# Larger pieces for kept depthwise outputs, half-height band loads, and a schedule that counts a transfer's packets

## The chip, the core and the metric

The kernel runs on one core of one Trainium2 chip, in one launch. The metric is the device time of an execution in microseconds (us); the kernel before takes 2142.71 us (median of three runs). Engines are named as in the profile: PE is TensorE, whose weight loads (PEld) overlap its matmuls, DVE is VectorE, ACT is ScalarE, POOL is GpSimd, and SP is SyncE, which issues every DMA of this program.

## What is computed

The program is a decoder trunk of two layers over 1024 tokens of width 1024, all in float32. Layer 0 mixes tokens with a causal convolution module, layer 1 with windowed attention. Each layer then has a squared-ReLU MLP and a gated embedding. The change lies in the convolution module:

```python
def conformer_conv(x, w_in, b_in, w_dw, b_dw, ln_g, ln_b, w_out, b_out):
    h = x @ w_in + b_in
    a, gate = jnp.split(h, 2, axis=-1)
    h = a * jax.nn.sigmoid(gate)
    h = lax.conv_general_dilated(
        h, w_dw[:, None, :], window_strides=(1,), padding=[(CONV_WIDTH - 1, 0)],
        dimension_numbers=("NWC", "WIO", "NWC"), feature_group_count=D_MODEL) + b_dw
    h = jax.nn.silu(layer_norm(h, ln_g, ln_b))
    return h @ w_out + b_out
...
        x = layer_norm(DEEPNORM_ALPHA * x + y, mix_ln_g[i], mix_ln_b[i])
        x = layer_norm(DEEPNORM_ALPHA * x + sq_relu_mlp(x, mlp_w_up[i], mlp_w_down[i]),
                       mlp_ln_g[i], mlp_ln_b[i])
        x = x + (p[i] @ ple_w_proj[i]) * jax.nn.sigmoid(x @ ple_w_gate[i])
```

The depthwise convolution has 31 taps (CONV_WIDTH) for each of 1024 channels.

## The kernel before

**Precision and products.** Every operand is split in two parts (`wh`/`wl` for weights, `xh`/`xl` for activations), a rounded one that ACT writes and the rest that DVE writes. A product is three matmuls (`mm3`).

**The convolution stage.** Channels are worked in eight groups `c` of 128. For each group `conv_in(c)` multiplies by `w_in` (for `c` from 3 on by `conv_seven(c)`, seven half products in place of eight), applies the gate and calls `hand_over(c, h, g)` for each half `h` of the tokens: the gated half is split into a `zz` tile (for the last half of the last group a `wh` tile) and written to scratch memory `scr` in eight DMAs of 64 KB. `taps(c)` then does the depthwise convolution on PE. For each of two halves `jj` of the group's channels it loads two tiles `B` back from `scr`, and for each of them two bands of weights from `w_dw`. A band comes through a `z` tile of 576 columns. ACT rounds it into a band tile `E`, DVE writes the remainder for partitions 0 to 63 beside it, and nine matmuls of 256 columns use the two (in the profile `ps<-B,E`). There are 64 bands. The host lays each band out twice, for partitions 0 to 63 and again for 64 to 127.

**Kept outputs.** After a half group, four transposes bring its result into a PSUM tile `tr` with tokens on partitions. For the first seven groups (`c < KEPT`) one copy moves it to a `t` tile, on DVE for `jj` 0 and on ACT for `jj` 1, and one DMA writes that to `kept` in DRAM, 2 KB for each partition. At group 7 the outputs come back in 16 DMAs into tiles `X` (groups 0 to 3) and `A` (groups 4 to 6), one for each of the eight token tiles and each of the two. `kept` is ordered by group, half and token tile, so such a read collects pieces of 64 elements (256 bytes).

**What follows.** `conv_ln` takes the statistics of each token tile on DVE, normalizes on POOL (`X<-X,sm` and `A<-A,sm` in the profile), transposes on PE and applies Silu on ACT. `mix_out` multiplies by `w_out`. The embedding product `embed(0, ...)`, 96 matmuls which depend on none of this (`ps<-wh,wh`, `ps<-wl,wh`, `ps<-wh,wl`), stands between the taps and `conv_ln` in the program and is spread over both.

**Who sets the order.** The program is recorded as a list of operations, and `Recorder.schedule` writes each engine's instruction order from it by list scheduling: priorities follow the order of recording, shifted by `later`, and each operation gets a planned duration (`cost`). For a DMA the plan has one queue. A transfer begins 1400 ns after its issue at the earliest, occupies the queue for its elements divided by 75 ns, and its data are there 2800 ns after the issue at the earliest. Tiles come from pools with few slots (`SLOTS`: 4 of `z`, 5 of `t`, 1 of `zz`, 6 of `ps`, 2 of `tr`); an operation that needs a slot waits until the slot's last user is done. On the chip each engine runs its order as written and waits at semaphores, so what stands behind a waiting instruction on its engine waits too. The DMAs use eight completion semaphores in turn, so SP issues a DMA only when the one eight places earlier has landed. All operations are recorded through one line, L466 (L471 in the changed kernel), so the profile is read by tile names.

Of the kernel before, what the change touches and what calls it, by code (L numbers as in the profile page):

```python
# [10 lines left out]
F32 = mybir.dt.float32  # L11
F32R = mybir.dt.float32r
AF = mybir.ActivationFunctionType
ALU = mybir.AluOpType

P = 128
# [4 lines left out]
HT = 512  # L21
# [11 lines left out]
PH = 4  # L33
# [19 lines left out]
KEPT = 7  # L53
# [69 lines left out]
class View:  # L123
# [30 lines left out]

    def to_broadcast(self, shape):
        return View(self.buf, np.broadcast_to(self.idx, shape[1:]), self.parts, self.steps + (("bro", shape),))

    def real(self):
        a = self.buf.tile
# [37 lines left out]
class Recorder:  # L197
# [120 lines left out]
    def schedule(self):  # L318
        import heapq

        for o in self.ops:
            o.deps.pop(o, None)
            o.left = len(o.deps)
            for x in o.deps:
                x.outs.append(o)
        engs = ("tensor", "vector", "scalar", "gpsimd", "sync")

        held = dict(vector=0.0, gpsimd=0.0)

        def both(o):  # L330
            if o.eng == "gpsimd":
                return o.name != "memset" and o.outv[0].n > 8
            if o.eng != "vector":
                return False
            if o.name == "tensor_copy":
                src = o.allv
            else:
                src = [v for k, v in o.kw.items() if k in ("in0", "in1") and isinstance(v, View)]
            return len(src) > 1 and not any(v.buf.space == "PSUM" for v in src)

        free = dict.fromkeys(engs, 0.0)
        fut = {e: [] for e in engs}
        rdy = {e: [] for e in engs}
        table = 0
        dma = 0.0
        order = []
        lat = 200.0
        same = dict(vector=127.0, scalar=93.0, gpsimd=100.0)

        def delay(o, x):  # L350
            a, b = o.eng, x.eng
            if a in ("alloc", "sync") or b == "alloc":
                return 0.0
            if a == b:
                return same.get(a, 0.0)
            return 200.0 if a == "tensor" else 260.0 if b == "tensor" else 150.0

        def enable(o):
            if o.eng == "alloc":
                return  # L360
            for e in ("vector", "gpsimd") if o.eng == "either" else (o.eng,):
                heapq.heappush(fut[e], (o.ready, o.prio, o.num, o))

        def finish(o, end):
            o.end = end
            order.append(o)
            for x in o.outs:
                r = end + delay(o, x) + (0.0 if o.eng in ("tensor", "alloc") else x.slack)
                if r > x.ready:
                    x.ready = r  # L370
                x.left -= 1
                if x.left == 0:
                    enable(x)
            for b in o.bufs:
                b.users -= 1
                b.end = max(b.end, end)
                if b.users == 0 and b.slot is not None:
                    heapq.heappush(self.tags[b.tag]["free"], (b.end + lat, b.slot))
                    serve(b.tag)

        def serve(tag):
            t = self.tags[tag]
            q = t["queue"]
            while q and t["free"]:
                o = q.pop(0)
                ft, s = heapq.heappop(t["free"])
                o.alloc.slot = s
                if o.name == "move":
                    dst = o.args[1]
                    heapq.heappush(self.tags[dst]["free"], (ft, s))  # L390
                    finish(o, ft)
                    serve(dst)
                else:
                    finish(o, ft)

        for o in self.ops:
            if o.eng == "alloc":
                self.tags[o.alloc.tag]["queue"].append(o)
        for t in self.tags:
            serve(t)  # L400
        for o in self.ops:
            if o.left == 0 and o.eng != "alloc" and not o.deps:
                enable(o)
        while True:
            best = None
            for e in engs:
                while rdy[e] and rdy[e][0][2].end:
                    heapq.heappop(rdy[e])
                while fut[e] and fut[e][0][3].end:
                    heapq.heappop(fut[e])  # L410
                if rdy[e]:
                    t = free[e]
                elif fut[e]:
                    t = max(free[e], fut[e][0][0])
                else:
                    continue
                if best is None or t < best[0]:
                    best = (t, e)
            if best is None:
                break  # L420
            t, e = best
            while fut[e] and fut[e][0][0] <= t:
                r, p, i, o = heapq.heappop(fut[e])
                if not o.end:
                    heapq.heappush(rdy[e], (p, i, o))
            p, i, o = heapq.heappop(rdy[e])
            if WAIT and fut[e] and e != "tensor":
                r, p2, i2, o2 = fut[e][0]
                if not o2.end and r <= t + WAIT and p2 < p - 300:
                    heapq.heappush(rdy[e], (p, i, o))  # L430
                    heapq.heappop(fut[e])
                    t, o = r, o2
            if o.eng == "either":
                o.eng = e
                o.dur = self.cost(o, o.outv, o.allv)
            d = o.dur
            if e == "scalar" and o.name == "activation":
                k = TABLE.get(o.args[2].name if len(o.args) > 2 else "", 0)
                if k and k != table:
                    table = k  # L440
                    d += 1283.0
            if both(o):
                d += max(0.0, held["gpsimd" if e == "vector" else "vector"] - 50.0 - t)
                held[e] = t + d
            free[e] = t + d
            if e == "sync":
                v = o.allv[0]
                dma = max(dma, t + 1400.0) + v.n * v.parts / 75.0
                finish(o, max(dma, t + 2800.0))
            else:  # L450
                finish(o, t + d)
        assert len(order) == len(self.ops), (len(order), len(self.ops))
        self.length = max(free.values())
        return order
# [44 lines left out]
class Emit:  # L499
# [318 lines left out]
    def conv(self):  # L818

        nc, d, ws = self.nc, self.d, self.ws  # L820
# [13 lines left out]
        Z = {}  # L834
# [138 lines left out]
        def taps(c):  # L973
# [3 lines left out]
            for jj in range(2):  # L977
                pss = [self.ps() for k in range(2)]
                for j in range(2):
# [3 lines left out]
                    nc.sync.dma_start(G2[:, :, HIST : HIST + U], scr[c, 2 * jj + j].rearrange("p (k u) -> p k u", k=2))  # L983
                    exchange = nc.ops[-1]
                    for k in range(2):
                        w = nc.tile("z", (P, n))
                        nc.sync.dma_start(w, d["w_dw"][c, jj, 2 * j + k])
                        w = w.rearrange("p (m q) -> p m q", q=PH * CG)
                        e = bands[turn[0] % len(bands)]
# [2 lines left out]
                        if e in fresh:  # L992
                            fresh.remove(e)
                            nc.gpsimd.memset(ev.bitcast(F32)[LOW, :, 1, :], 0.0)
                        nc.scalar.copy(ev[:, :, 0, :], w)
                        nc.vector.tensor_tensor(
                            out=ev[HIGH, :, 1, :], in0=w[HIGH], in1=ev[HIGH, :, 0, :].bitcast(F32), op=ALU.subtract
                        )
                        for i in range(SHIFTS):
                            o = k * LO + HIST - i  # L1000
# [23 lines left out]
                        nc.tensor.transpose(pv[:, h, j], y[:, o : o + P], self.ident)  # L1024
                nc.slack = 0.0
                if c < KEPT:
                    s = self.sb("t")
                    (nc.scalar.copy if jj else nc.vector.tensor_copy)(s, pt)
                    nc.sync.dma_start(kept[:, (2 * c + jj) * HT : (2 * c + jj + 1) * HT], s)
                    yield  # L1030
                    continue
                if c == KEPT and jj == 0:
                    kv = kept.rearrange("p (c s u) -> p c s u", c=2 * KEPT, s=2 * PH)
                    for q in range(2):
                        m = min(8, 2 * KEPT - 8 * q)
                        for h in range(2):
                            for f in range(PH):
                                Z[h, f, q] = self.sb("XA"[q])
                                dst = Z[h, f, q][:, 0 : 64 * m].rearrange("p (c u) -> p c u", u=64)
                                with nc.later(BACK_BY):  # L1040
                                    nc.sync.dma_start(dst, kv[:, 8 * q : 8 * q + m, PH * h + f, :])
                for h in range(2):
                    for f in range(PH):
                        o = c % 4 * P + jj * 4 * CG
# [43 lines left out]
            forms()  # L1088
        more_bands()
        kept = self.dram("kept", 2 * KEPT * HT)  # L1090
        ins = (x for c in range(8) for x in conv_in(c))
        outs = (x for c in range(8) for x in taps(c))
        for n in range(32 + LAG):
# [902 lines left out]
def layout(a):  # L1996
# [9 lines left out]
    r = {}  # L2006
# [21 lines left out]
    for q in range(CG):  # L2028
        band[:, :, :, :, q, :, q] = wt[:, :, :, :, q, :]
    band = band.reshape(8, 2, 4, P // 2, SHIFTS * PH * CG)  # L2030
    r["w_dw"] = c(np.concatenate([band, band], axis=3))

    bd = np.asarray(a["conv_b_dw"])[0].reshape(32, 2, CG).transpose(2, 1, 0).reshape(CG, 64)
    r["cconst"] = c(
# [45 lines left out]
```

## Time and profile before

| | before |
|---|---|
| median of 3 runs | 2142.71 us (2142.64 to 2142.78) |
| the profiled execution's own time | 2142.3 us |
| its span in the trace | 2140.5 us |
| PE busy | 2116.5 us, 99% |
| DVE, ACT, POOL busy | 1757.5, 1152.3, 280.6 us |
| moved by DMA | 462.46 MB in 228939 packets, mean 216 GB/s |
| packets under 512 bytes | 38192 |

The span runs from the first to the last instruction of one profiled execution; the execution's own time has 1.8 us around that. Busy time of PE is the union of its matmuls, each of which is drawn with its full latency (389 ns for 512 columns) although the next one starts after some 226 ns; a short delay between two matmuls therefore does not show as idle time.

### The profile page before, as it was taken

What the parts mean: (1) busy time and instruction counts of PE and PEld (TensorE: products, weight loads), DVE (VectorE), ACT (ScalarE), POOL (GpSimd) and SP (SyncE); (2) the same over time, 40 slices, a digit from 0 to 9 for tenths busy, and PEclk for the clock granted to TensorE, in tenths of its full rate; (3) what the DMA queues carried; (4) which work ended last, traced back from release to release, by engine and by line L of the source; (5) the groups of instructions that cost most, each with busy time, mean ns of one, the idle gap of its engine ahead of it and who ended that gap; (6) DMA issues with size and microseconds to landing.
All of it is one profiled execution on the core that took longest, in us unless ns stands there. A gap on an engine that the chain in (4) does not pass through costs nothing.

```text
span 2140.5 us, 29992 instructions
## 1 busy us (share of the span) xinstructions
PE 2116.5 (99%) x10008; PEld 1752.9 (82%) x10008; DVE 1757.5 (82%) x2854; ACT 1152.3 (54%) x2146; POOL 280.6 (13%) x495
## 2 busy tenths in 40 slices
PE   9999899999999999999999999999999999999999
PEld 7888778888888888888788888888888888888877
DVE  6866579988898788876986888689988988788688
ACT  5655554654544633335755888445445554333484
POOL 0000052200000000001320656240000000000042
PEclk9999999999999999999999999999999999999999
DMA  9877965867786756655487022665778795565726
GB/s 295 234 203 203 268 245 177 285 222 250 264 271 231 278 177 204 201 184 213 156 284 249 11 89 79 208 239 184 257 267 296 262 332 174 179 233 170 262 75 230
DMA packets 228939, 462.46 MB, mean 216 GB/s; under 512 B 38192, under 2 KB 64432, under 8 KB 228784
## 3 DMA queue, kind: packets, MB, share of 16 engines
q1 hardware_dynamic: 228784, 460.54, 65.1%
q8 instruction: 79, 1.29, 0.2%
q14 instruction: 76, 0.62, 0.1%
HBM read 312.34 MB, written 148.11 MB: 215 GB/s over the span
## 4 chain that ended last, share of the span: by engine, by line
PE 40%; DVE 5%; ACT 3%; DMA 2%; issue 1%; POOL 1%; SPq 0%; POOLq 0%; DVEq 0%; ACTq 0%
PE ps L466 31%; PE tr L466 9%; DVE xl L466 1%; DMA t<-proj 1%; ACT z L466 1%; DVE t L466 1%; POOL sm L466 1%; DVE z L466 1%; DVE sm L466 0%; DVE A L466 0%; DVE B L466 0%; ACT xh L466 0%; DMA raw<-in_w_kv_dram 0%; ACT t L466 0%; DMA raw<-gate_t 0%
## 5 line engine op out<-in xcount | busy, mean ns | idle before, releaser
L466 PE MATMUL ps<-xh,xl 128*128 128x512 f32 x636 | 247.6, 389 | 0.0
L466 PE MATMUL ps<-xh 128*128 128x512 f32 x636 | 247.6, 389 | 0.0
L466 PE MATMUL ps<-xl,xh 128*128 128x512 f32 x636 | 247.6, 389 | 0.0
L466 ACT CAST wh<-raw 128x1024 fp32r<-128x1024 f32 (+2 forms) x156 | 143.4, 923 | 134.7 <-PE ps L466 84.0
L466 POOL TENSOR_SCALAR sm<-sm 128x1 f32<-128x1 f32 x72 | 28.3, 397 | 1364.0 <-DVE E L466 612.0
L466 PE MATMUL ps<-xl,wh 128*128 128x512 f32 x508 | 198.7, 392 | 0.0
L466 PE MATMUL ps<-xh,wl 128*128 128x512 f32 x508 | 198.3, 391 | 0.0
L466 PE MATMUL ps<-xh,wh 128*128 128x512 f32 x508 | 196.1, 392 | 0.9 <-ACT xh L466 0.9
L466 PE MATMUL ps<-wh,xh 128*128 128x512 f32 (+1 forms) x404 | 159.2, 395 | 1.7 <-ACT zz L466 0.9
L466 PE MATMUL ps<-wh,xl 128*128 128x512 f32 (+1 forms) x404 | 160.4, 397 | 0.0
L466 PE MATMUL ps<-wl,xh 128*128 128x512 f32 (+1 forms) x404 | 159.3, 394 | 0.0
L466 ACT CAST wh<-g 128x512 fp32r<-128x512 f32 x128 | 76.4, 620 | 153.8 <-PE ps L466 73.7
L466 ACT CAST xh<-wh 128x1024 fp32r<-128x1024 f32 x76 | 79.7, 1049 | 118.0 <-PE tr L466 90.4
L466 PEld LDWEIGHTS ps<-xl,xh 128*128 128x128 f32 x636 | 119.4, 188 | 24.9
L466 PEld LDWEIGHTS ps<-xh,xl 128*128 128x128 f32 x636 | 119.4, 188 | 24.7
L466 PEld LDWEIGHTS ps<-xh 128*128 128x128 f32 x636 | 119.5, 188 | 24.6
L466 DVE TENSOR_TENSOR wl<-raw,wh 128x1024 fp32r<-128x1024 f32 (+1 forms) x100 | 100.0, 1001 | 35.5 <-ACT wh L466 35.1
L466 DVE TENSOR_TENSOR xl<-wh,xh 128x1024 fp32r<-128x1024 f32 x76 | 92.8, 1221 | 25.6 <-ACT xh L466 25.6
L466 PEld LDWEIGHTS ps<-xh,wh 128*128 128x128 f32 x508 | 95.4, 188 | 22.5 <-ACT xh L466 1.6
L466 PEld LDWEIGHTS ps<-xh,wl 128*128 128x128 f32 x508 | 95.5, 188 | 19.5
L466 PEld LDWEIGHTS ps<-xl,wh 128*128 128x128 f32 x508 | 95.4, 188 | 19.5 <-DVE xl L466 1.3
L466 DVE TENSOR_TENSOR wl<-g,wh 128x512 fp32r<-128x512 f32 x128 | 84.6, 686 | 26.8 <-ACT wh L466 26.8
(447 smaller groups left out, 5620.0 us busy)
## 6 DMA issues: line engine op xcount, KB each, us to landing
wh<-hid SPq DMA_DIRECT2D x78, 512.0 KB, 4.1
raw<-in_w_up_dram SPq DMA_DIRECT2D x61, 512.0 KB, 4.3
wl<-in_w_down_dram SPq DMA_DIRECT2D x58, 512.0 KB, 4.8
hid<-zz SPq DMA_DIRECT2D x96, 256.0 KB, 4.0
z<-in_w_dw_dram SPq DMA_DIRECT2D x64, 288.0 KB, 4.0
hid<-t SPq DMA_DIRECT2D x70, 256.0 KB, 3.0
raw<-hid SPq DMA_DIRECT2D x30, 512.0 KB, 3.7
B<-scr SPq DMA_DIRECT2D x32, 256.0 KB, 4.5
```

What stands on the lines that cost most here:

```text
L466: getattr(getattr(nc, o.eng), o.name)(*a, **k)
```

## The change

Four things change in the kernel, and the order of all engines with them.

1. A band is laid out once by the host (64 rows) and loaded once, into a `z` tile of 64 partitions. ACT copies it twice, to partitions 0 to 63 (`HIGH`) and to 64 to 127 (`LOW`) of the band tile.
2. A kept output is copied from PSUM in two halves (`h` 0 on DVE, `h` 1 on ACT), into two `t` tiles that are taken at `jj` 0 and filled at `jj` 1. Two DMAs for each group then write them, in pieces of 128 elements (512 bytes), to a `kept` that is ordered by token tile, group and channel.
3. The 16 reads of `kept` are then one contiguous run for each partition (2048 or 1536 bytes).
4. `schedule` charges a transfer by the larger of its two sides: 9 ns for each contiguous piece and 0.0366 ns for each byte, over 16 engines.

```diff
+    def transfer(self):
+
+        i = self.idx.ravel()
+        pieces = self.parts * (1 + int((np.diff(i) != 1).sum()))
+        return (9.0 * pieces + 0.0366 * 4 * i.size * self.parts) / 16
...
             if e == "sync":
-                v = o.allv[0]
-                dma = max(dma, t + 1400.0) + v.n * v.parts / 75.0
+                dma = max(dma, t + 1400.0) + max(v.transfer() for v in o.allv)
                 finish(o, max(dma, t + 2800.0))
...
-                        w = nc.tile("z", (P, n))
+                        w = nc.tile("z", (P // 2, n))
                         nc.sync.dma_start(w, d["w_dw"][c, jj, 2 * j + k])
...
-                        nc.scalar.copy(ev[:, :, 0, :], w)
+                        for rows in (HIGH, LOW):
+                            nc.scalar.copy(ev[rows, :, 0, :], w)
                         nc.vector.tensor_tensor(
-                            out=ev[HIGH, :, 1, :], in0=w[HIGH], in1=ev[HIGH, :, 0, :].bitcast(F32), op=ALU.subtract
+                            out=ev[HIGH, :, 1, :], in0=w, in1=ev[HIGH, :, 0, :].bitcast(F32), op=ALU.subtract
                         )
...
                 if c < KEPT:
-                    s = self.sb("t")
-                    (nc.scalar.copy if jj else nc.vector.tensor_copy)(s, pt)
-                    nc.sync.dma_start(kept[:, (2 * c + jj) * HT : (2 * c + jj + 1) * HT], s)
+                    for h in range(2):
+                        if jj == 0:
+                            wait[h] = self.sb("t")
+                        v = wait[h].rearrange("p (f j u) -> p f j u", f=PH, j=2)
+                        src = pt[:, h * 256 : (h + 1) * 256].rearrange("p (f u) -> p f u", f=PH)
+                        (nc.scalar.copy if h else nc.vector.tensor_copy)(v[:, :, jj, :], src)
+                        if jj:
+                            dst = kept.rearrange("p (s c u) -> p s c u", s=2 * PH, c=KEPT)
+                            nc.sync.dma_start(dst[:, PH * h : PH * h + PH, c, :], wait[h].rearrange("p (f u) -> p f u", f=PH))
                     yield
                     continue
                 if c == KEPT and jj == 0:
-                    kv = kept.rearrange("p (c s u) -> p c s u", c=2 * KEPT, s=2 * PH)
                     for q in range(2):
-                        m = min(8, 2 * KEPT - 8 * q)
+                        m = min(4, KEPT - 4 * q)
                         for h in range(2):
                             for f in range(PH):
                                 Z[h, f, q] = self.sb("XA"[q])
-                                dst = Z[h, f, q][:, 0 : 64 * m].rearrange("p (c u) -> p c u", u=64)
+                                o = ((PH * h + f) * KEPT + 4 * q) * P
                                 with nc.later(BACK_BY):
-                                    nc.sync.dma_start(dst, kv[:, 8 * q : 8 * q + m, PH * h + f, :])
+                                    nc.sync.dma_start(Z[h, f, q][:, 0 : P * m], kept[:, o : o + P * m])
...
-    r["w_dw"] = c(np.concatenate([band, band], axis=3))
+    r["w_dw"] = c(band)
```

More of the change, by code (lines that the diff above doesn't have):

```diff
@@ L1090, in conv @@
         kept = self.dram("kept", 2 * KEPT * HT)
+        wait = {}
         ins = (x for c in range(8) for x in conv_in(c))
```

## The prediction

> **What bounds the kernel now.** I read the busy times first, then the same by stretches of 100 us, since a share over the whole span would hide a bad stage.
>
> ```profile
> span 2140.5 us, 29992 instructions
> PE 2116.5 (99%) x10008; PEld 1752.9 (82%) x10008; DVE 1757.5 (82%) x2854; ACT 1152.3 (54%) x2146; POOL 280.6 (13%) x495
> ```
>
> ```profile
> 0.00:100.00 100.00, 97.02 (x479) 81.12 (x480) 76.34 (x117) 59.91 (x101) 3.56 (x20) 1.00 0.87 265
> 200.00:300.00 100.00, 91.57 (x517) 77.44 (x516) 66.00 (x119) 58.10 (x110) 25.73 (x38) 0.98 0.96 290
> 500.00:600.00 100.00, 100.00 (x443) 82.42 (x442) 89.59 (x141) 50.91 (x87) 0.00 (x0) 1.00 0.79 259
> 1000.00:1100.00 100.00, 96.75 (x462) 78.78 (x462) 85.93 (x147) 70.23 (x126) 33.73 (x40) 1.00 0.46 159
> 2000.00:2140.50 140.50, 134.22 (x630) 110.43 (x628) 109.82 (x178) 85.56 (x147) 38.72 (x43) 0.99 0.55 186
> ```
>
> The columns after the stretch and its length are busy us (and instructions) of PE, PEld, DVE, ACT and POOL, the granted PE clock, the DMA share and GB/s. PE bounds the kernel: it idles 2140.5 - 2116.5 = 24.0 us in all. In a full stretch it starts 443 matmuls of 512 columns, one every 100/443 = 0.226 us. The change removes no matmul, so it can win only idle time. Of that 8.4 us lie in 200 to 300, at the end of the convolution stage, the fullest stretch for DMA (0.96) and the place where the kept outputs return. The next two views take it apart.
>
> ```profile
> 220.00:230.00 10.00, 10.00 (x61) 8.80 (x60) 6.65 (x11) 5.58 (x8) 1.33 (x4) 1.00 1.15 263
> 230.00:240.00 10.00, 7.51 (x49) 6.69 (x48) 8.13 (x12) 5.35 (x11) 0.00 (x0) 0.84 1.00 290
> 240.00:250.00 10.00, 7.04 (x30) 5.23 (x31) 6.13 (x9) 6.11 (x11) 0.00 (x0) 0.98 0.91 246
> 270.00:280.00 10.00, 8.16 (x45) 6.21 (x45) 8.75 (x24) 6.87 (x13) 9.67 (x14) 1.00 0.95 329
> 280.00:290.00 10.00, 9.11 (x49) 6.74 (x48) 6.93 (x13) 7.34 (x15) 9.51 (x13) 1.00 1.04 399
> ```
>
> ```profile
> PE ps L466 <- ACT xh L466: 2.5, 2, 1.6
> PE ps L466 <- DVE E L466: 2.1, 2, 1.1
> PE ps L466 <- POOL X L466: 1.8, 1, 1.8
> PE ps L466 <- DVE g L466: 1.7, 2, 1.2
> PE tr L466 <- POOL X L466: 1.0, 3, 0.4
> ```
>
> The second view lists whom PE waited for in the first 320 us (total, times, longest). There are two troughs. At 230 to 250 PE loses 2.49 + 2.96 = 5.45 us, to bands (`E`) and to the evacuation queue; at 270 to 290 it loses 1.84 + 0.89 = 2.73 us to POOL's normalization. With the 3 us of the first stretch, all within the change's direct reach is some 11 us, half a per cent.
>
> The trough also costs clock: 0.84 granted over 10 us is (1 - 0.84) x 10 / 0.5 = 3.2 us at half speed, 1.6 us of work lost. The Trainium skill ("TensorE: Matmul & The Clock Gate", Part 1) says that the clock halves after an idle window of about 3.4 us, in steps of such windows; the trace agrees with the size of one step, though the longest single wait here is under 2 us. By that rule a longer wait would cost at least the same step again; I charge it once below from the row.
>
> **The change, part by part.**
>
> *Reads of `kept` and band loads.* The reads go from 256-byte pieces to one run; each band load halves.
>
> ```profile
> z<-in_w_dw_dram SPq DMA_DIRECT2D x12, 288.0 KB, 4.4
> B<-scr SPq DMA_DIRECT2D x8, 256.0 KB, 4.9
> kept<-t SPq DMA_DIRECT2D x4, 256.0 KB, 4.6
> scr<-wh SPq DMA_DIRECT2D x8, 64.0 KB, 2.2
> ```
>
> These are landings at 210 to 270 us. The stretch 220:230 moves 263 GB/s at a share of 1.15, 229 GB/s per full share; 280:290, with long pieces only, moves 399 at 1.04, 384. The 16 reads (8 of 256 KB, 8 of 192 KB, 3.67 MB) therefore free about 3.67/0.229 - 3.67/0.384 = 6.5 us of DMA time. A band load of 144 KB should land between the rows of 64 and 288 KB, at about 2.2 + (80/224) x 2.2 = 3.0 us, 1.4 us sooner. With that and the freed queue the 2.1 us of waits for `E` go. Before this trough DMA time hides behind PE, so the saved band bytes win nothing more there.
>
> *ACT's second copy.*
>
> ```profile
> 20.00:250.00 230.00, 223.98 (x1237) 193.80 (x1236) 165.51 (x242) 132.32 (x232) 5.37 (x32) 0.99 0.82 235
> L466 ACT CAST E<-z 128x576 fp32r<-128x576 f32 x64 | 42.6, 667 | 14.6 <-DMA z<-in_w_dw_dram 8.8 <-PE ps L466 3.0 <-PE tr L466 2.3
> L466 DVE TENSOR_TENSOR E<-z,E 64x576 fp32r<-64x576 f32 x64 | 47.2, 746 | 39.4 <-ACT E L466 26.9 <-PE ps L466 12.3
> ```
>
> DVE's band operation takes 746 ns on 64 partitions, so I charge a half-height copy in full: 64 x 0.667 = 42.6 us, bringing ACT from 132.3 to 174.9 of 230 us (76%). DVE needs only the HIGH copy, so the LOW one (667) runs beside DVE's 746 and a band is ready no later. I take 0, with +4 us as the bound if ACT's slack doesn't hold. The 14 evacuations become 28 of half width, split as before: nothing on PE.
>
> *Kept writes.* Two `t` tiles of five stay taken for a whole half group, and the gate's activation of the next group waits for a slot that the write must free, with ACT's bands and casts behind it. In ACT's new order three to five operations stand between (about 2 to 3.3 us at 0.62 to 0.67) against a landing of 4.6; PE has work. 0 here, in a rival below.
>
> *The tail of the taps.* Here the order changes, which I read from the built programs. Both run 54 band matmuls after the last convolution product. Before, 36 embedding matmuls (one of them behind the transposes) follow and then the last group's 72 band matmuls in a row. Now only 10 embedding matmuls stand ahead, the other fillers later.
>
> ```profile
> 222.25 5.31 SPq L466 DMA_DIRECT2D X<-kept  x4
> 228.74 4.46 PE L466 MATMUL ps<-B,E 128*128 128x256 f32 x36
> 230.84 3.95 SPq L466 DMA_DIRECT2D kept<-t  x1
> 232.18 0.67 DVE L466 TENSOR_TENSOR t<-t,ps 128x512 f32<-128x512 f32 x1
> 232.89 0.69 DVE L466 TENSOR_TENSOR t<-t,t 128x512 f32<-128x512 f32 x1
> 233.62 0.62 ACT L466 CAST wh<-t 128x512 fp32r<-128x512 f32 x1 [0.36 <-DVE t L466]
> 234.88 0.68 DVE L466 TENSOR_TENSOR wh<-t,wh 128x512 fp32r<-128x512 f32 x1
> 236.34 4.31 SPq L466 DMA_DIRECT2D scr<-zz  x8
> 241.22 3.71 SPq L466 DMA_DIRECT2D scr<-wh  x8
> 246.89 1.89 SPq L466 DMA_DIRECT2D B<-scr  x3
> 252.07 8.77 PE L466 MATMUL ps<-B,E 128*128 128x256 f32 x72
> ```
>
> Before, SP is held twice (5.31 and 3.95 us), and the last tiles `B` are asked for 18 us after the last product. The chain's parts are the hand-over (0.67 + 0.69 + 0.62 + 0.68 = 2.7, with hops about 3.5), sixteen issues (4.31 + 3.71 = 8.0) and a landing (4.9): the first `B` is there 16.4 us after the product, or 6.8 + 8.0 + 4.9 = 19.7 if the hand-over is as late as before (235.56 - 228.74). PE gets there after 54 x 0.122 + 10 x 0.226 + 0.5 = 9.4 us. So the trough of 5.45 us becomes one wait of 7.0 us, up to 10.3; if the emptier queue lands `B` as fast as `scr` (2.2), 4.3. I take 6.0, and the clock's 1.6 as before: +0.5 us, from -2.8 to +5.
>
> *Normalization.* Taps and POOL move forward together. Before its first transposes PE has 22 fillers after the last tap transposes in place of 28 (6 x 0.226 = 1.4 us less cover), then 31 in place of 26 among the next 32 transposes (1.1 more). I take +0.5 (from -2.7, the whole idle, to +3).
>
> *The start.* The plan now believes in faster transfers, and the first band stands after 176 matmuls, not 221.
>
> ```profile
> 41.40 3.96 SPq L466 DMA_DIRECT2D scr<-zz  x8
> 47.49 2.61 SPq L466 DMA_DIRECT2D B<-scr  x4
> 55.16 2.31 PE L466 MATMUL ps<-B,E 128*128 128x256 f32 x18
> ```
>
> That is 45 x 0.226 = 10.2 us earlier, at 45.0. The product it depends on ends 29 matmuls (6.5 us) earlier, so `B` is asked for at 41.0 and lands at 45.9: PE waits 0.9 us. If `B` isn't asked for earlier at all (47.49 + 4.9 - 45.0), 7.4. I take +1.0 (0 to +7.4).
>
> *The rest.* Attention (1000 to 1400) is reordered too, as its plan starts from other times; the MLP's PE order hardly changes, and PE is full there. I see no sign: 0, within 3 us either way (idle is 3.25 us in 1000:1100, 6.3 in the last stretch).
>
> The sum is 0.5 + 0.5 + 1.0 = +2 us, with the 0.5 that I lean toward loss in the rest, +2.5: a profiled execution of 2142.3 + 2.5 = 2144.8. The median lies 0.4 us above the profiled time, so **2145.2 us**.
>
> **The rivals.** What a measurement of this kernel tells from no change I set at 0.2%, 4.3 us: faster is below 2138.4, slower above 2147.0.
>
> *The relief wins.* Waits for `E` go, SP is never held, `B` lands early, and taps and POOL run forward with more filler behind them. For it: DMA at or over a full share exactly where PE idles. Against it: the fillers are spent later. It gives 2.8 us in the tail, 2.7 us in normalization and 1 us more if the clock never drops, about -6: 2137. Chance 0.18.
>
> *Hidden anyway.* The reads are smaller transfers beside a full PE, and the new order happens to fit; troughs of the same size in other places: 2142.5, within 2. Chance 0.12.
>
> *The plan trusts DMA too far (slower).* One mechanism: band matmuls stand ahead of the time when their `B` tiles land, and PE cannot pass them. At both ends at the bounds: 7.4 at the start, 10.3 + 1.6 - 7.05 = 4.9 at the tail: +12, 2155. It decides from about 2 us of lateness at both ends over my values. For it: shares of 0.87 to 1.15 at both places, so a plan by undisturbed packets is too early there. Half of it gives 2149. Chance 0.28.
>
> *ACT (slower).* At 76%, with the seven waits for kept writes of up to 2 us each (14 us) it would be at 189 of 230, and PE would wait some 0.6 us for each of seven groups and the 0 to 4 us above: +6, 2149. Against it: ACT's longest waits now are for PE, not the other way. Chance 0.10.
>
> **How the numbers follow.** My forecast has 0.32 (2142 to 2148 by itself). Faster is the first rival, 0.18; same is the forecast and the hidden case, 0.44; slower is the last two, 0.38. The range runs from the relief's value to the slow rival's, short of its extreme: 2137 to 2154, leaving out somewhat under 0.2.
>
> **What would show it.** Right: in the changed profile no waits of PE for `E` near 230, the last 72 band matmuls starting near 245 after one wait of 4 to 7 us with the clock below 1 there, ACT near 175 us between 20 and 250, a first band between 45 and 47, and PE's idle sum near 26. Wrong: a PE without troughs up to 310 (relief), PE waiting for ACT in the middle of the stage (ACT), or an idle sum that grows most in 1000 to 1400, which I gave no sign.

## The result, and the profile after

| | before | after |
|---|---|---|
| median | 2142.68 us | 2195.18 us (2188.93 to 2199.58, 4 runs) |
| profiled execution: own time, span | 2142.3, 2140.5 us | 2196.05, 2194.2 us |
| PE busy, idle | 2116.5, 24.0 us | 2135.2, 59.0 us |
| time in which PE's granted clock is 0.5 | 7.9 us | 33.6 us |

The changed kernel is slower by 2.4% (ratio 1.0243, 95% interval 1.0218 to 1.0268). The forecast was 2145.2 us in a range of 2137 to 2154. The time lies 41 us above that range. The page of the changed kernel begins:

```profile
span 2194.2 us, 30087 instructions
PE 2135.2 (97%) x10008; PEld 1761.5 (80%) x10008; DVE 1760.6 (80%) x2856; ACT 1194.6 (54%) x2217; POOL 290.5 (13%) x500
DMA packets 217932, 453.03 MB, mean 206 GB/s; under 512 B 23856, under 2 KB 58288, under 8 KB 217776
```

DVE's work is unchanged (1760.6 against 1757.5 us) and ACT's grew by the 42 us that were forecast. DMA moves 9.4 MB less, in fewer small packets. The work is as planned, so the time is in the waits. The span grew by 53.7 us. PE idle grew by 35.0. The clock accounts for at most (33.6 - 7.9) / 2 = 12.9 us of PE's longer busy time (part of the half-speed time falls into waits or behind the last matmul), and the other 5.8 or more are delays too short to show as idle time. The stretches of the changed kernel (columns as in the prediction) tell where:

```profile
0.00:100.00 100.00, 89.52 (x414) 74.36 (x415) 66.37 (x102) 62.41 (x105) 3.45 (x19) 0.95 0.75 216
200.00:300.00 100.00, 87.22 (x502) 74.84 (x501) 61.19 (x107) 69.79 (x129) 15.37 (x31) 0.97 0.85 248
500.00:600.00 100.00, 100.00 (x441) 82.39 (x441) 88.81 (x141) 50.60 (x86) 0.00 (x0) 1.00 0.75 250
1100.00:1200.00 100.00, 91.14 (x429) 74.47 (x427) 68.23 (x128) 55.01 (x110) 19.53 (x8) 0.98 0.78 267
```

Before, the first stretch held 479 matmuls, now 414. The stretch from 1100 to 1200, to which the prediction gave nothing as a part of the attention, had PE busy 99.12 us (507 matmuls) and has 91.14 (429). By then the changed kernel is over 30 us behind, so the same stretch does not hold the same work. A way to place the whole loss is to take the start of the n-th matmul in both traces, since the two programs have the same 10008 (in an order that differs in part):

| n-th matmul (when, in the changed kernel) | 250 (71 us) | 1000 (205) | 1250 (256) | 2250 (474) | 5250 (1154) | 5500 (1218) | 8000 | 10000 |
|---|---|---|---|---|---|---|---|---|
| later than before, us | 12.4 | 13.8 | 21.9 | 26.8 | 33.2 | 44.1 | 50.4 | 54.0 |

There are three steps (the start 12.4, the tail of the taps 8.1, the set-up of attention 10.9), and between them a slow drift through both MLPs. By matmul 250 the changed kernel has run 36 of the short band matmuls and the kernel before 25, so the start's true loss is about 1 us more. The next rows are the start in the changed kernel's timeline (start, duration, engine, operation, in brackets the wait ahead of it and what ended it):

```profile
38.10 7.16 SPq L471 DMA_DIRECT2D scr<-zz  x8
46.31 1.26 SPq L471 DMA_DIRECT2D B<-scr  x2
50.00 3.85 PE L471 MATMUL ps<-B,E 128*128 128x256 f32 x18 [5.22 <-ACT B L471]
54.52 0.69 DVE L471 TENSOR_TENSOR g<-g,g 128x512 f32<-128x512 f32 x1 [3.23 <-DMA g<-in_xT_dram]
64.34 2.26 PE L471 MATMUL ps<-B,E 128*128 128x256 f32 x9 [3.61 <-DVE E L471]
```

PE reaches the first band after fewer fillers (176 matmuls, as the prediction read from the order, not 221) and waits 5.22 us; `B` was asked for only 3.7 us before. SP had needed 7.16 us to issue the eight writes of `scr` ahead of it, where it needed 3.96 before. The row names an ACT cast, but that writes another tile of the pool `B` and ends at 49.86; the load of `B` landed at 49.87, 3.56 us after its issue, and PE went on at 50.00. The 18 matmuls then take 3.85 us instead of 2.31, because the clock is at half from 49.9 to 53.3. DVE waits 3.23 us for a load of tokens, with band operations behind that in its queue, and PE waits 3.61 us for the next band, with the clock at half again from 63.5 to 70.4. At the tail of the taps the wait is on DVE as well:

```profile
235.93 0.69 DVE L471 BATCH_NORM_STATS2 sm<-X 128x6 f32<-128x512 f32 x1 [8.70 <-DMA X<-kept]
240.66 0.69 DVE L471 BATCH_NORM_STATS2 sm<-X 128x6 f32<-128x512 f32 x1 [2.64 <-DMA X<-kept]
242.78 1.11 PE L471 MATMUL tr<-ident,g 128*128 128x128 f32 x4 [4.67 <-DVE g L471]
```

The statistics of two outputs read back stand in DVE's queue before the work that PE needs next. DVE waits 8.70 and 2.64 us for the reads, and PE 4.67 us behind it, with the clock at half for 6.8 us from 241.0. At the attention's set-up one group tells it, the 24 casts on ACT that split weights (busy time and mean duration, then ACT's idle time ahead of them and what ended it). The first row is the kernel before, the second the changed one:

```profile
L466 ACT CAST X<-X 128x512 fp32r<-128x512 f32 x24 | 14.5, 625 | 1.1 <-DMA X<-in_w_o_dram 1.1
```

```profile
L471 ACT CAST X<-X 128x512 fp32r<-128x512 f32 x24 | 14.8, 624 | 19.5 <-DMA X<-in_w_q_dram 12.2 <-DMA w_q<-X 4.7 <-DMA w_o<-X 2.4
```

The casts cost the same. ACT used to be handed these weights when they had landed; now it stands waiting 19.5 us for them. What stands behind such a cast on ACT comes late to PE:

```profile
1169.33 0.62 ACT L471 CAST X<-X 128x512 fp32r<-128x512 f32 x1 [2.96 <-DMA X<-in_w_q_dram]
1170.12 0.38 ACT L471 COPY t<-ps 128x256 f32<-128x256 f32 x1
1172.03 0.41 PE L471 MATMUL ps<-ident,t 128*128 128x128 f32 x2 [2.09 <-DVE t L471]
```

The copy of `ps` to `t`, on which DVE and then PE's transposes depend, had to let the cast pass first. And PE's waits over the whole changed kernel (total, times, longest), where the longest sum before was 2.6:

```profile
PE ps L471 <- ACT t L471: 10.7, 12, 2.6
PE ps L471 <- DVE t L471: 6.5, 8, 2.1
PE ps L471 <- ACT B L471: 5.2, 1, 5.2
PE tr L471 <- DVE g L471: 4.7, 1, 4.7
PE ps L471 <- DVE E L471: 3.6, 1, 3.6
```

By name PE waits for DMAs 2.7 us in all, and the row of 5.2 us is the load of `B` told above. For the rest it waits for the other engines, DVE and ACT above all, and in the places shown here these wait for DMAs that their written order expects earlier.

### The profile page after: what moved, and what is told of

It reads as the page before. It is cut to its first block, busy times and chain, and to the rows that moved or that the text cites. A ratio compares the mean times of both kernels' runs of the same rounds, so it can differ in the third digit from the quotient of the medians.

```text
span 2194.2 us, 30087 instructions
## 1 busy us (share of the span) xinstructions
PE 2135.2 (97%) x10008; PEld 1761.5 (80%) x10008; DVE 1760.6 (80%) x2856; ACT 1194.6 (54%) x2217; POOL 290.5 (13%) x500
## 4 chain that ended last, share of the span: by engine, by line
PE 33%; DMA 7%; DVE 6%; ACT 4%; issue 2%; POOL 0%; SPq 0%; ACTq 0%; DVEq 0%; POOLq 0%
PE ps L471 25%; PE tr L471 8%; DVE xl L471 2%; DMA hid<-zz 1%; ACT z L471 1%; DMA raw<-gate_t 1%; DMA w_q<-X 1%; ACT wh L471 1%; DVE t L471 1%; DVE zz L471 1%; DMA raw<-in_w_q_dram 1%; DVE wl L471 1%; DMA raw<-in_w_kv_dram 1%; DVE z L471 1%; DMA form<-t 1%
## 5 line engine op out<-in xcount | busy, mean ns | idle before, releaser
L471 PE MATMUL ps<-wh,xh 128*128 128x512 f32 x496 | 199.1, 402 | 4.3 <-ACT zz L471 1.8
L471 PE MATMUL ps<-wl,xh 128*128 128x512 f32 x496 | 198.2, 400 | 1.0 <-DMA wl<-gate_low_t 1.0
L471 PE MATMUL ps<-wh,xl 128*128 128x512 f32 x496 | 198.1, 400 | 0.0
L471 PEld LDWEIGHTS ps<-wh,xh 128*128 128x128 f32 x496 | 94.4, 190 | 23.6 <-ACT zz L471 2.6
```

Of the source, the lines that this page charges most:

```text
L471: getattr(getattr(nc, o.eng), o.name)(*a, **k)
```

## The experiments

Kernels run together share their runs of the kernel before (medians 2143.39, 2143.40, 2143.56 and 2142.50 us for the four groups).

**The price and the data apart.** The first four separate the edit of `schedule` from the three edits of data, and ask whether any other order would cost as much.

```diff
 e1: the changed kernel with the old price
-                dma = max(dma, t + 1400.0) + max(v.transfer() for v in o.allv)
+                v = o.allv[0]
+                dma = max(dma, t + 1400.0) + v.n * v.parts / 75.0
 e2: the kernel before with the new price
-                v = o.allv[0]
-                dma = max(dma, t + 1400.0) + v.n * v.parts / 75.0
+                dma = max(dma, t + 1400.0) + max(v.transfer() for v in o.allv)
 e3 and e4: the kernel before
-                dma = max(dma, t + 1400.0) + v.n * v.parts / 75.0
+                dma = max(dma, t + 1400.0) + v.n * v.parts / 76.0        (e4: / 97.5)
```

> The changed kernel with the schedule's old price of a transfer (elements of the first operand divided by 75 ns); the half-height bands and the larger kept pieces stay. If the new price in the schedule makes the loss (theory P), this stands near the kernel before: 2136 to 2150 us, with the first wait for a tile B at the start under 1 us. If the data changes make it, ACT's 64 added copies above all (theory D), 2180 to 2200. If any disturbance of the written order costs as much (theory O), 2160 to 2200, in places that have nothing to do with transfers.

> The kernel before with only the schedule's price of a transfer changed (pieces and bytes). Theory P: the loss is here, 2180 to 2200 us, with a first band product 8 to 10 us earlier in the order and a wait of some 5 us in front of it. Theory D: 2140 to 2148. Theory O: 2160 to 2200.

> The kernel before with 76 in place of 75 in the schedule's price of a transfer, a disturbance of 1.3%. Theory O: the order changes in many places and the time with it, 2160 us or more. Theory P: 2141 to 2147, since the price stays near what transfers take beside others. Theory D says nothing against 2143.

> The kernel before with 97.5 in place of 75: a load of 256 KB is charged 672 ns as by the new price, pieces are not counted. Theory P: most of the loss, 2170 to 2200 us. If it is the counting of pieces that matters (which makes kept reads and scratch reads dearer than bytes alone), it differs from the plan-only kernel by over 10 us. Theory D: near 2143.

Measured: e1 2145.72 us (ratio 1.0010, 1.0001 to 1.0019), e2 2181.84 (1.0181, 1.0165 to 1.0196), e3 2140.11 (0.9984, 0.9974 to 0.9993), e4 2184.79 (1.0194, 1.0178 to 1.0209). So the price alone costs 38 us and the data alone 2: theory P holds, and theories D and O fall (e3 lies 0.9 us below P's range, far from O's). What matters in the price is its rate: e4 charges 256 KB with the 672 ns of the new price, counts no pieces, and loses 41 us. Half-speed time is 3.5 us in e1, 22.5 in e2 and 31.9 in e4. The start of e4 shows the late band by name:

```profile
52.31 3.90 PE L466 MATMUL ps<-B,E 128*128 128x256 f32 x18 [7.23 <-DMA B<-scr]
```

**Which data change adds to the price.** 38 and 2 do not make 52.

```diff
 e7: e2, and of the data changes the half-height bands alone
 e8: e2, and of the data changes the order of kept alone
```

> The kernel before with the new price and the half-height band loads alone; kept outputs as before. The price alone gave 2181.8, price and both data changes 2195.2. If the bands make the difference (their load is charged 373 ns where it was 983, so DVE and ACT operations stand still earlier in their queues): 2190 to 2197. If the kept outputs do: 2180 to 2185.

> The kernel before with the new price and the new order of the kept outputs alone; bands loaded twice as before. If the kept outputs make the difference between 2181.8 and 2195.2 (reads charged 590 to 670 ns after gaps of pieces are gone, so the tail of the taps is planned earlier): 2188 to 2197. If the bands do: 2180 to 2186, with most of the later matmuls in the start gone.

Measured: 2186.03 us (1.0196, 1.0181 to 1.0211) and 2185.23 (1.0193, 1.0178 to 1.0208). By the totals neither change is the one: e7 lies between its two expectations, e8 at the edge of the second, and each adds some 4 us. By place they differ. Matmul 250 is late by 5.7 us in e2, 12.2 in e7, 5.4 in e8 and 12.4 in the changed kernel, so the start's extra loss comes with the bands. Between matmuls 1000 and 1250 the losses are 0.8, 3.9, 5.9 and 8.1 us, as if at the tail both added. That is not shown: these are single executions, and e9 below, which has the changed kernel's orders up to 300 us, stands 2.8 us better than it at matmul 250. The last 6 us of the total stay unassigned.

**Does each stage pay for its own price?**

```diff
 e9: the changed kernel
-                dma = max(dma, t + 1400.0) + max(v.transfer() for v in o.allv)
+                v = o.allv[0]
+                cost = max(v.transfer() for v in o.allv) if t < 300e3 else v.n * v.parts / 75.0
+                dma = max(dma, t + 1400.0) + cost
```

> The changed kernel with the new price only for transfers whose planned issue lies before 300 us (the convolution stage); the old price afterwards. The profile of the changed kernel loses 26.8 us to matmul 2250 (about 520 us) and 27.2 us behind it. Theory A (each stage pays for its own price): the first part stays and the second goes: matmul 2250 is 20 to 28 us late, the last about as much, in all 2163 to 2174. Theory B (what is late early stays in disorder for the rest, as every order follows from the one before it): the second part stays too, 2182 or more.

Measured: 2162.86 us (1.0091, 1.0074 to 1.0108). Matmul 2250, which the changed kernel reaches at 474 us (the expectation has about 520), is 21.3 us late and matmul 10000 21.4. Theory A holds: nothing is lost after 300 us once the old price is back, and the attention's stretch is full again.

```profile
1100.00:1200.00 100.00, 98.60 (x486) 80.83 (x485) 69.93 (x161) 62.73 (x147) 9.40 (x14) 1.00 0.80 279
```

So the 27 us behind matmul 2250 in the changed kernel belong to the price of transfers that no edit of data touches. e2, which has none of the data edits, loses 29.6 us there.

**Rate or latency.**

```diff
 e5: the changed kernel, 256 KB in 874 ns again
-        return (9.0 * pieces + 0.0366 * 4 * i.size * self.parts) / 16
+        return (9.0 * pieces + 0.0366 * 4 * i.size * self.parts) / 16 * 1.3
 e6: the changed kernel
-                dma = max(dma, t + 1400.0) + max(v.transfer() for v in o.allv)
-                finish(o, max(dma, t + 2800.0))
+                dma = max(dma, t + 2800.0) + max(v.transfer() for v in o.allv)
+                finish(o, max(dma, t + 4200.0))
 e12: both edits
```

> The changed kernel with the new price times 1.3: pieces and bytes counted as in the change, but 256 KB are charged 874 ns as before the change, not 672. Theory R (the rate: the plan lets the queue move more bytes than it does under load): the loss goes, 2138 to 2148 us, with half-clock time under 8 us. Theory L (the latency: the plan believes data land 2.8 us after the issue, the trace shows 3 to 5): the floors stay, so at least half of the loss stays, 2165 or more. Theory C (counting pieces is what disturbs the order, whatever the level): 2180 or more.

> The changed kernel at its new price, with the plan's two floors raised by 1.4 us (transfer begins 2800 ns after its issue at the earliest, data there after 4200). Theory R: each isolated load is planned later, but a full queue is still too fast, so less than half of the loss goes: 2168 or more. Theory L: planned landings are then near the measured 3 to 5 us, and the loss goes: 2140 to 2155.

> The changed kernel with both corrections: the new price times 1.3 (2149.5 alone), and the floors raised by 1.4 us (2164.9 alone, where the price was left as in the change). If rate and latency are two parts of the same lateness of the plan, correcting both gives the least: 2137 to 2147, with the first band not waited for. If the rate alone matters and a higher floor only disturbs: 2148 to 2158.

Measured: e5 2149.48 us (1.0028, 1.0018 to 1.0037), e6 2164.87 (1.0096, 1.0081 to 1.0111), e12 2148.96 (1.0027, 1.0016 to 1.0037). The rate alone takes back 46 of the 52 us (1.5 us beyond what was expected of it), and its half-speed time, 17.1 us, is twice what was expected. The floors alone take back 30, so neither theory's bounds hold for e6: latency counts too. Both together are no better than the rate alone, as the second expectation of e12 had it.

**The other side of the price.**

```diff
 e11, e10, e15: the changed kernel with the old price, divided by another rate
-                dma = max(dma, t + 1400.0) + v.n * v.parts / 75.0
+                dma = max(dma, t + 1400.0) + v.n * v.parts / 65.0        (e10: / 76.0; e15: / 74.0)
```

> The changed kernel with the old price, divided by 65 (256 KB in 1008 ns): the plan trusts DMA less than before. If the loss grows with the price's error on one side only (a late landing is paid, an early one only costs a slot): 2138 to 2150, with half-clock time under 8 us. If the price of 75 is a narrow optimum and any deviation of 13% costs the like: 2155 or more.

> The changed kernel with the old price, divided by 76 instead of 75 (256 KB in 862 ns instead of 874). The data changes alone gave 2145.7, the kernel before with 76 gave 2140.1. If the 3 us of the latter belong to the price: 2139 to 2144. If they are what any small change of the order gives by chance: anywhere within 2139 to 2150, and not with that sign.

> The changed kernel with the old price divided by 74: with 75 it gave 2145.7, with 76 2149.5. Scatter of the order by chance: anywhere within 2141 to 2152. A trend of the price: 2142 to 2145.

Measured: e11 2158.92 us (1.0072, 1.0057 to 1.0087), e10 2149.54 (1.0023, 1.0013 to 1.0033), e15 2151.41 (1.0044, 1.0029 to 1.0059). Two things follow. A price that trusts DMA too little costs as well, as the second expectation of e11 had it, though less: 13 us over e1 for a price 15% higher, where one 23% lower cost 38 to 49. And a change of the price by 1.3% either way moves the time of the same data by 4 to 6 us with no trend, so differences of that size between two orders are the chance of an order and say nothing of price or data. That holds for e3 too: its 3 us below the kernel before, the best time found, did not come back when the same 76 was used with the changed data. With the old price between 74 and 76 the data changes cost 2 to 9 us and gain in none of the three kernels.

**Lateness by itself.** The last pair keeps the old rate and shifts every planned landing of the kernel before by the same amount.

```diff
 e13 and e14: the kernel before
-                finish(o, max(dma, t + 2800.0))
+                finish(o, max(dma, t + 2800.0) - 1100.0)        (e14: + 1100.0)
```

> The kernel before with its old price, every planned landing 1.1 us sooner. Theory M (what counts is how far ahead of the measured landing the plan believes the data to be there): the share of transfers planned over 1 us too early rises from 0.2 to about 0.5 in the middle of the program, but in the full stretches (start, end of the convolution stage) the plan keeps the 4 us by which it expects data too late: those stay, the MLP and attention lose, in all 2152 to 2172. Theory Q (the rate alone): under 2149.

> The kernel before with its old price, every planned landing 1.1 us later. Theory M: nothing is planned too early that was not before, so 2138 to 2149, with half-clock time under 10 us. Theory N (the tuned order is a narrow optimum, and any shift of this size costs as much): 2152 or more, as with the shift the other way.

Measured: e13 2165.41 us (1.0115, 1.0100 to 1.0130), e14 2150.34 (1.0038, 1.0024 to 1.0053). Planning every landing 1.1 us sooner than the old price does costs 23 us, within theory M's range; 1.1 us later costs 8, which is 1 us over what theory M expected and under theory N's 2152, near the chance of an order. The half-speed time of e14, 11.9 us, is over the 10 expected. The start of e13 stays good:

```profile
48.52 2.72 SPq L466 DMA_DIRECT2D B<-scr  x4
55.48 2.31 PE L466 MATMUL ps<-B,E 128*128 128x256 f32 x18
```

Its matmul 250 is 0.3 us late. Theory M had the end of the convolution stage stay good too, but matmul 1250 is 8.0 us late. The larger part of the loss comes later, in the second MLP: 8.1 us at matmul 6000, 21.6 at 9000.

**Plan and trace side by side.** Building a program gives for each DMA the issue and the landing with which `schedule` wrote the order. SP issues the same 1475 DMAs in that order, so the k-th of the plan can be set beside the k-th of the trace. "Early" is the share of DMAs that took over 1 us longer from issue to landing than planned. The last column takes those issued in the first 60 us.

| kernel | planned mean, us | measured mean | early | median time, us | first 60 us: planned, measured |
|---|---|---|---|---|---|
| before | 5.21 | 4.44 | 0.21 | 2142.7 | 8.67, 4.51 |
| e1, data, old price | 5.06 | 4.47 | 0.22 | 2145.7 | 8.12, 4.83 |
| e5, new price x 1.3 | 4.93 | 4.45 | 0.23 | 2149.5 | 8.54, 5.12 |
| e14, 1.1 us later | 6.22 | 4.46 | 0.03 | 2150.3 | 9.09, 4.62 |
| e11, data, / 65 | 6.88 | 4.39 | 0.08 | 2158.9 | 10.27, 4.82 |
| e6, floors raised | 4.82 | 4.41 | 0.16 | 2164.9 | 5.89, 4.85 |
| e13, 1.1 us sooner | 4.25 | 4.50 | 0.51 | 2165.4 | 8.10, 4.70 |
| e2, price alone | 3.68 | 4.41 | 0.51 | 2181.8 | 5.22, 4.65 |
| after | 3.46 | 4.38 | 0.53 | 2195.2 | 4.72, 4.89 |

The measured mean is 4.4 to 4.5 us whatever the plan believes; the page's medians say the same, here for two groups before and after:

```profile
raw<-in_w_up_dram SPq DMA_DIRECT2D x61, 512.0 KB, 4.3
hid<-zz SPq DMA_DIRECT2D x96, 256.0 KB, 4.0
```

```profile
raw<-in_w_up_dram SPq DMA_DIRECT2D x61, 512.0 KB, 4.2
hid<-zz SPq DMA_DIRECT2D x96, 256.0 KB, 4.1
```

Two different things are lost. The old price overcharges a full queue: at the start it expects 8.67 us where 4.51 pass, and this is a margin. The new price takes that margin away (4.72 against 4.89, nearly right on average). In the seven kernels whose plan has 4.7 to 5.9 us there, matmul 250 is 5.4 to 12.4 us late; in the nine others, whose rate is the old one, near it or slower, 8.1 to 10.3 us are planned and it is between 0.4 us early and 5.0 late. The 5.0 is e10's, with 8.1 planned, so the margin alone does not settle it.

The set-up of attention, matmuls 5250 to 5500, had such a margin too: 5.75 us planned against 4.56 measured before. After the change it is 3.04 against 4.64, with 0.70 of the DMAs early. e13 still plans 5.35 us there and loses 2.9 us, not 10.9.

Much of the MLPs had no margin. Between matmuls 6000 and 8000 the old plan has 3.65 us against 4.05 measured, 0.26 early, and the new one 2.94, near its floor of 2.8, with 0.52 early and 5.5 us lost. e13 shows such early plans by themselves: 0.66 early there, 9.6 us lost. The share is not a price, though: between 2250 and 4000 e13 has 0.63 early and loses 1.0.

The Trainium skill ("DMA: Bandwidth & Descriptors", Anatomy of one DMA) fits 2.0 us and 436 GB/s to a DMA on the path that GpSimd issues: 2.6 us for 256 KB and 3.2 for 512 KB by that law, which is an estimate. The plan after the change lies near it (3.46 us on the mean), and the trace does not agree: 4.0 to 4.3 us in the rows above, issued by SP with other transfers under way. GpSimd's own path was not run here.

## Why the prediction was wrong

**The step that failed** is the one headed "The rest": "Attention (1000 to 1400) is reordered too, as its plan starts from other times; the MLP's PE order hardly changes, and PE is full there. I see no sign: 0, within 3 us either way." It is 27.2 us behind matmul 2250, all of it the price (e9). The sign was there and not weighed: `schedule` charges every transfer of the program, and the prediction's own rows gave landings of 4.4 to 4.9 us for its large transfers, where the new plan believes in 2.8 (its median; 3.77 before). The prediction looked at PE's order. In the first MLP that hardly changes, as it said; in the attention the orders of all engines do, and there the loss came through ACT and DVE, whose orders it compared only around the taps. How much an order moves is no sign of loss either. In the fifth eighth of each engine's list, which lies in the attention, e2 moves about 0.3 of PE's operations, 0.5 of DVE's and 0.4 of ACT's against the kernel before, and e3, which loses nothing, moves as many.

**The rival named the mechanism and sized it wrongly.** "The plan trusts DMA too far" was right in kind. It was bounded at +12 us because it was given two places, PE in front of `B`. At the start the bound was 7.4 us; the waits there were 5.22 and 3.61 us, and with the clock and short delays the stretch lost 12.4. The first is the wait that the forecast sized at 1.0: `B` was to be asked for at 41.0 and was asked for at 46.31. The second wait was for a band behind a load on DVE, not for `B`. At the tail the bound was +4.9; 8.1 were lost, by PE's wait of 4.67 us behind statistics on DVE (8.70 and 2.64 us) and the half speed that goes with it, which is not the place foreseen. The wait for the last `B`, charged with 6.0 us, was 0.4 by name.

**The clock** was charged once, 1.6 us. It came to 33.6 us at half speed in six steps of 3.4 or 6.8 us and one of 2.9 at the very end of the program, at most 12.9 us more work lost than before. The prediction quoted the Trainium skill ("TensorE: Matmul & The Clock Gate", Part 1) on this; its steps of about 3.4 us agree with the trace (3.41 and 6.83), and every single wait of PE of 3.6 us or more in the rows above has one that begins in it.

**Tail of the taps and normalization**, +0.5 each: the tail cost 8.1 us, and another 4.9 went between matmuls 1250 and 2250 (256 to 474 us), where the normalization lies and the first MLP begins.

**ACT's second copy**, 0 with +4 as the bound. The price of one was right:

```profile
L471 ACT CAST E<-z 64x576 fp32r<-64x576 f32 x108 | 71.3, 670 | 5.3 <-DMA z<-in_w_dw_dram 2.4 <-PE ps L471 1.6
```

That is 670 ns at half height, in the copies between 20 and 250 us, against 667 at full. All data changes together cost 2 us in e1 and up to 9 at a neighbouring price, so ACT is no bound, as argued, though the 0 cannot be told from a few us of chance.

**Reads of `kept` and band loads.** The band loads in the stretch from 210 to 270 us landed in 3.8 us where 3.0 was worked out (4.4 before), and the reads were no faster, 7.0 against 6.2 us into `X` and 5.6 against 5.3 into `A`, though their pieces are up to eight times as long. In e1 they took 6.8 and 4.4 us. The first row is before, the others after:

```profile
X<-kept SPq DMA_DIRECT2D x8, 256.0 KB, 6.2
```

```profile
z<-in_w_dw_dram SPq DMA_DIRECT2D x15, 144.0 KB, 3.8
X<-kept SPq DMA_DIRECT2D x8, 256.0 KB, 7.0
```

The saving in DMA time is seen (share 0.87 in 200 to 300 of e1, whose pace is that of before, against 0.96), but there was nothing to be won by it: PE waited for `E` 2.6 us in all before. PE's waits for `E`, which were to go there, came back between 190 and 300 as 2.7 us on ACT's part of `E`.

**Kept writes** at 0: ACT waits 1.9 us for them between 20 and 250, which fits.

**The signs.** Of those named for being right, four did not come: the first band stands at 50.0 us, not between 45 and 47; the last 72 band matmuls, no longer in a row, begin at 265.0, not near 245; ACT is busy 155.5 us between 20 and 250, not 175; and PE's idle sum is 59.0, not 26. For being wrong it named "an idle sum that grows most in 1000 to 1400, which I gave no sign". That came in part: idle time grew by 10.1 us there, 8.0 of it in 1100 to 1200, more than in any other 100 us; in 0 to 300 it grew by 12.5.

## What to carry to other kernels

An edit of one number in a planner is an edit of the whole program: compare the orders of all engines over the whole span, and set the plan's times beside the trace's, transfer by transfer, before giving the rest of the program a zero. Where engines run a written order, a price for DMA should be what the loaded queue takes plus a margin, since landings planned 1.1 us sooner, which on the mean was nearly right (4.25 us planned, 4.50 measured), cost 23 us here and landings planned 1.1 us later cost 8. A more exact charge for pieces that lowers the rate's level is not an improvement, and a time that differs by 0.3% or less after a 1% change of a planner's constant proves nothing of the constant.

## What the runs showed of the hardware

- Time from issue to landing hardly depends on the order or the price: 4.36 to 4.50 us on the mean in the seventeen kernels of this study, with a tenth of the DMAs over 6.5 to 6.9 us.
- Reading `kept` in runs of 1536 to 2048 bytes in place of 256-byte pieces did not shorten its landing in the changed kernel (7.0 against 6.2 us into `X`, 5.6 against 5.3 into `A`). In e1 the reads into `A` took 4.4 us and those into `X` 6.8. Why they differ was not tried apart, nor an empty queue.
- In the changed kernel a single PE wait of 3.6 to 5.2 us brought 3.4 or 6.8 us at a granted clock of 0.5, beginning in the last 1.8 us of the wait or less. Over the whole program at most 12.9 us more went this way than before, beside 35.0 us of added idle time.
